# Cross-attention stage of a one-core encoder step: weight loads queued later, staging and operand buffers moved, first two score products no longer interleaved

## The chip, the core and the metric

The kernel runs on one core of one Trainium2 chip. The metric is the device time of one execution in microseconds (us). The kernel before takes 2992.53 us, the median of 3 runs (2989.19 to 2996.63). The names of the engines are those of the profile: PE is the matrix engine, DVE the vector engine, ACT the scalar engine, POOL the general engine, SP the engine that issues most of the transfers. Operands live in on-chip memory (SBUF), sums of matmuls in a small second memory (PSUM), the large arrays in DRAM.

## The reference

One layer of an encoder on 2048 prompt rows (16 tiles of 128 rows) and 128 sample rows (one more tile, S). Three sub-layers follow one another, each with a norm before and after it and an addition to its input:

```python
x = x + rmsnorm(mixer(rmsnorm(x, g_mix_pre)), g_mix_post)          # attention over a band, convolution, projection
x = x + rmsnorm(memory_attention(rmsnorm(x, g_mem_pre)), g_mem_post)  # 4 heads into 256 memory tokens
x = x + rmsnorm(ffn(rmsnorm(x, g_ffn_pre)), g_ffn_post)            # SwiGLU, hidden 2816

def memory_attention(h, mk, mv, w_mq, w_mo):
    q = (h @ w_mq)                                  # per head
    s = einsum("bthd,bmhd->bhtm", q, mk) * MEM_HEAD_DIM ** -0.5
    p = softmax(s, axis=-1)
    return einsum("bhtm,bmhd->bthd", p, mv) @ w_mo
```

## The kernel before, in words

The stages run one after another: memory keys and values, input projection, band attention, output projection of the mixer (`mixout`), cross attention (`phase_cross`), the first half of the feed-forward layer (`gate_up`) and the second (`down`). A tile scheduler puts the program's instructions into one list for each engine; an engine works through its list strictly in order and waits at each instruction for what that instruction needs. A buffer is a place in memory that a pool hands out in rotation, and an instruction that writes a buffer waits until the last reader of whatever lay at that place has finished. So two names that share a place are tied to each other even where no data passes between them.

A float32 product is made of three products of "high" and "low" parts. `mm3h` (L286 to L292) gives, for one 128-row slice k of the operands, six matmuls 128x512; a product of a tile with a 1024x1024 matrix is eight slices, 48 matmuls, all at L291.

**The end of `mixout` (L1030 to L1063).** It takes tile S and then tiles 0 to 15. For each it loads a tile of x (L1036), runs 48 matmuls, squares (ACT L1053), a small sum and a power on POOL (L1054, L300, L301), scales by the norm on DVE (L1057) into the single buffer `po`, adds x on POOL (L1058) and stores the result x1 by a transfer from POOL (L1059). Between these matmuls stands the whole cross attention of the sample rows (`cross_sample`), whose last piece is `postnorm` (L334 to L341: ACT L308, POOL L300 and L301, DVE L339, POOL L340, store L341). It uses the same buffer `po`.

**`phase_cross`.** Folded weights are kept in DRAM: `f1s` for the scores, `f2s` for the values, eight blocks each. `load` (L1207) brings one block into a staging buffer `stg` (there are three), ACT makes its high part (L1212), and DVE, or POOL for blocks 1, 3 and 5 of `f1`, makes the low part (L1213). `norm(t)` loads tile t of x1 (L1218) and runs `prenorm`: ACT square (L308), POOL L300 and L301, DVE scaling into the single buffer `hn` (L315), eight transposes on PE (L318) into the PSUM place `t`, the high part by ACT (L319), the low part by DVE (L320). `scores` makes 48 matmuls into a PSUM place, then a maximum on DVE (L1230), four exponentials on ACT (L1234), a reciprocal (L1237) and four scalings (L1239). `probs` transposes the result on PE (L1245) into the same place `t` and splits it (ACT L1248, DVE L1249). `values` makes 48 matmuls and calls `postnorm`.

In the steady part the program order for tile t is: transposes of the probabilities of t, scores of t+1, norm of t+2, values of t. From t = 4 on, `natural` (L1263 to L1285) is called once a tile as long as there is work for it: it takes two finished tiles of the cross stage and prepares the operands of the feed-forward stage. It loads the two tiles into `na` and `nb` (L1270), squares (ACT L1273), POOL L1275 and L1276, scales each (DVE L1277), makes four differences on POOL (L1278, L1280, L1282, L1284) and stores four pieces to the DRAM array `hn` with transfers that POOL issues (L1279 `na`, L1281 `nt`, L1283 `nb`, L1285 `na` again).

**The opening of `phase_cross`.** The program calls `norm(0)`, the eight loads of `f1`, `norm(1)`, `scores` of tile 0 into the PSUM place `y`, then two loads of `f2` behind the first exponentials, then `probs` and the scores of tile 1. The scheduler interleaves the scores of tiles 0 and 1.

**The opening of `gate_up`.** The first weights of the feed-forward layer come into four buffers `wf`; `wforms` derives four sums from them on POOL (L1372 to L1375), and splits seven forms on ACT (L1377) and DVE (L1378). `tform` loads pieces of `hn` and transposes them on PE (L1355; ACT L1357, DVE L1358). The products are L283, L284 and L285 (128x384).

**Places in memory.** The tables `lay(arena, start, (name, size, count))` and `at(name, size, (arena, [starts]))` give the places, in units of 1 KB a partition. In the float32 arena `sbF` of `phase_cross`: `stg` at 0, 4, 8; `gpre` 12; `junk` 16; `hn` 18; `xt` 22, 26, 30. `na`, `nb` and `nt` are laid at 0, 4, 8, over the staging buffers that are done by then. `gate_up` uses in the same arena `wf` at 12, 18, 46.5, 22, `s` (the derived sums) at 26, 28, 38.5, and `x1`, `x2` at 30, 31.5, 33, 34.5.

Of the kernel before, what the change touches and what calls it, by code (L numbers as in the profile page):

```python
# [20 lines left out]
NPT = 16  # L21
# [37 lines left out]
def halves(y):  # L59
    return [y[:, o, :] for o in range(2)]  # L60
# [76 lines left out]
class Build:  # L137
# [149 lines left out]
    def mm3h(self, y, lh, ll, rh, rl, start, stop):  # L287
        nc = self.nc
        for x, (l, r) in enumerate(((lh, rh), (lh, rl), (ll, rh))):
            for o in range(2):  # L290
                nc.tensor.matmul(y[o], l, r[:, o * 512:(o + 1) * 512], start=start and x == 0,  # L291
                                 stop=stop and x == 2)  # L292

    def rstd(self, pool, ss, scale):
        nc = self.nc
# [683 lines left out]
    def mixout(self, ctx):  # L979
# [52 lines left out]
        for i, t in enumerate(order):  # L1032
            mh, ml = ready.pop(t)
            pre = ahead(i)
            xt = self.t(pool, [P, D], F32, "xt", 2)
            nc.sync.dma_start(xt[:, :], self.rows("x", t))  # L1036
            y = [self.t(ps_y, [P, 512], F32, "y")[:, :] for _ in range(2)]
            for k in range(KC):
                self.mm3h(y, mh[:, k, :], ml[:, k, :], ws[k][0], ws[k][1], k == 0, k == KC - 1)
# [21 lines left out]
                fill, due = self.cross_sample(pool, ps_so, ps_p), 0.0  # L1061
        for _ in fill:
            pass  # L1063

    def cross_sample(self, pool, ps_so, ps_p):
        nc, A = self.nc, self.A
# [121 lines left out]
    def phase_cross(self, ctx):  # L1188
        nc, A = self.nc, self.A
        sbF, sbR = self.sbF, self.sbR  # L1190
        fr = Joined(*self.flex(ctx, *[(1024, F32R)] * 11))
        pool = (Region().lay(sbF, 0, ("stg", 4, 3), ("gpre", 4, 1), ("junk", 2, 1), ("hn", 4, 1), ("xt", 4, 3))
                .lay(sbF, 34.5, ("gpost", 4, 1), ("z", 4, 2), ("po", 4, 1), ("ss", 0.015625, 6),
                     ("rstd", 0.015625, 6), ("nmx", 0.03125, 2), ("sm", 0.03125, 2), ("ri", 0.03125, 2))
                .at("sh", 4, (sbR, [44, 40, 24])).at("sl", 4, (sbR, [52, 48, 28]))
                .lay(sbF, 0, ("na", 4, 1), ("nb", 4, 1), ("nt", 4, 1)))
        for k, o in enumerate((56, 64, 80, 0, 8, 16, 72, 88)):
            pool.lay(sbR, o, (f"f1{k}h", 4, 1), (f"f1{k}l", 4, 1))
        spots = [(sbR, o) for o in (32, 36, 96, 100, 104)] + [(fr, 4 * i) for i in range(11)]
        for i, (arena, o) in enumerate(spots):  # L1200
            pool.at(f"f2{i // 2}{'hl'[i % 2]}", 4, (arena, [o]))
        ps_t = ps_s = ps_y = (Region().at("y", 4, (self.ps, [4, 0])).lay(self.ps, 8, ("t", 4, 1), ("s", 4, 1)))
# [13 lines left out]
        def norm(t):  # L1216
            xt = self.t(pool, [P, D], F32, "xt", 4)
            nc.sync.dma_start(xt[:, :], self.x1[t])  # L1218
            hh = self.t(pool, [P, KC, P], F32R, "sh", 3)
            hl = self.t(pool, [P, KC, P], F32R, "sl", 3)  # L1220
            self.prenorm(pool, ps_t, xt, gpre, hh[:, :, :], hl[:, :, :], tag="t", keep=True)
            return xt, hh, hl

        def scores(hh, hl, where="s"):
            s = self.t(ps_s, [P, 2, 512], F32, where)
            for k in range(KC):
                self.mm3h(halves(s), hh[:, k, :], hl[:, k, :], f1[k][0], f1[k][1], k == 0, k == KC - 1)
            sv = s[:, :, :].rearrange("p a (h n) -> p (a h) n", n=NM)
            nmx = self.t(pool, [P, MH], F32, "nmx", 2)
            nc.vector.tensor_reduce(nmx[:, :], sv, axis=AX.X, op=ALU.max, negate=True)  # L1230
            z = self.t(pool, [P, MH, NM], F32, "z", 2)
            sm = self.t(pool, [P, MH], F32, "sm", 2)
            for h in range(MH):
                self.last_exp = nc.scalar.activation(z[:, h, :], sv[:, h, :], AF.Exp, bias=nmx[:, h:h + 1],  # L1234
                                                     accum_out=sm[:, h:h + 1])
            ri = self.t(pool, [P, MH], F32, "ri", 2)
            nc.vector.reciprocal(ri[:, :], sm[:, :])  # L1237
            for h in range(MH):
                nc.vector.tensor_scalar(z[:, h, :], z[:, h, :], ri[:, h:h + 1], None, ALU.mult)  # L1239
            return z  # L1240
# [21 lines left out]
        def natural(g, p):  # L1262
# [5 lines left out]
            for x, (t, r0) in zip((xa, xb), PAIRS[g][p][:2]):  # L1268
# [17 lines left out]

        self.natural = natural
        todo = [(g, p) for g in range(3) for p in range(3)]
        hq = {0: norm(0)}
        f1 = [load(self.f1s[:, k, :, :].rearrange("p h n -> p (h n)"), f"f1{k}",  # L1290
                   nc.gpsimd if k in (1, 3, 5) else nc.vector) for k in range(KC)]
        hq[1] = norm(1)
        z = scores(*hq[0][1:], "y")
        f2 = []

        def more(n, event):
            with self.tc.issue_after(event.ins):
                for k in range(len(f2), min(len(f2) + n, KC)):
                    f2.append(load(self.f2s[:, k, :], f"f2{k}"))

        more(F2, self.last_exp)
        for t in range(NPT):
            pp = probs(z) if t < NPT - 1 else self.last_probs
            if t == 0:
                more(KC, self.last_split)
            if t + 1 < NPT:
                z = scores(*hq[t + 1][1:])
            if t + 2 < NPT:
                hq[t + 2] = norm(t + 2)
            values(t, hq.pop(t)[0], *pp)  # L1310
            for g, p in list(todo):
                ready = all(x == S_TILE or x < t for x, _ in PAIRS[g][p][:2])
                if ready and t >= 4:
                    natural(g, p)
                    todo.remove((g, p))
                    break
# [333 lines left out]
```

## Time and profile before

| | |
|---|---|
| median of 3 runs | 2992.53 us (2989.19 to 2996.63) |
| the profiled execution, its own time | 2992.62 us |
| its span (first to last instruction) | 2990.8 us, mean granted clock of PE 0.987 |
| busy share of PE, DVE, ACT, POOL | 97%, 70%, 44%, 46% |
| norm of tile 0 to the end of the last values of the cross stage | about 1145 to 1566 us of the span |

A row of the timeline gives start, duration, engine, line, operation and what it writes and reads, and in brackets how long the engine had stood idle before it and what ended that. A row of the windows gives, for a stretch of the span, the busy time and number of instructions of each engine, the clock that PE was granted (1.00 is full speed), the share of the time in which the transfer engines moved data, and the rate. The waits give "engine, line <- what it waited for: total, times, longest" in us.

### The profile page before, as it was taken

To read this page: it belongs to the slowest core of one execution; us is meant where nothing else is said; L and a number is where in the kernel's file an instruction comes from. 1 tells how busy PE (TensorE), PEld (TensorE's weight loads), DVE (VectorE), ACT (ScalarE), POOL (GpSimd) and SP (SyncE) were. 2 spreads that over 40 slices of the span, in tenths; PEclk is the share of its full clock that TensorE was granted. 3 is DMA by queue.
4 is the path that set the end of the run, shared out by engine and by line. 5 is a ranking of instruction groups with operands and counts; after the bars stand their busy time and mean duration, and the time that the engine had idled before them with its cause. 6 is when DMAs were issued, how large, how long until landed. Compare 5 with 4: busy or idle time off the path is not lost.

```text
span 2990.8 us, 45392 instructions
## 1 busy us (share of the span) xinstructions
PE 2893.6 (97%) x16740; PEld 2636.6 (88%) x16740; DVE 2083.7 (70%) x3023; ACT 1314.1 (44%) x2665; POOL 1368.1 (46%) x1244
## 2 busy tenths in 40 slices
PE   8999999979989998999999999999999999999998
PEld 7999999959977777788878999999999999888786
DVE  6697895958975344435459878788888998555655
ACT  4535465648973223333334333433344444433433
POOL 0267496720013223135347656455556776424413
PEclk9999999989999999999999999999999999999999
DMA  8735255557844664224246333544434446756664
GB/s 300 247 115 176 97 167 159 176 151 189 207 134 157 233 212 169 71 88 146 96 156 218 132 126 131 187 144 159 148 128 150 150 145 213 241 171 221 220 193 165
DMA packets 198474, 500.04 MB, mean 167 GB/s; under 512 B 18981, under 2 KB 87085, under 8 KB 189923
## 3 DMA queue, kind: packets, MB, share of 16 engines
q1 hardware_dynamic: 187931, 461.09, 47.9%
q0 software_dynamic: 10320, 36.05, 3.1%
q8 instruction: 131, 2.15, 0.3%
q14 instruction: 92, 0.75, 0.1%
HBM read 365.97 MB, written 141.81 MB: 170 GB/s over the span
## 4 chain that ended last, share of the span: by engine, by line
PE 41%; DMA 4%; POOL 3%; DVE 2%; issue 2%; ACT 0%; DVEq 0%; SPq 0%; POOLq 0%; ACTq 0%
PE psb L285 13%; PE psb L284 13%; PE psb L283 13%; DMA sbf<-in_w_down_dram 1%; PE psb L291 1%; POOL sbf L1500 1%; DMA sbf<-x 1%; PE psb L1355 1%; DMA sbf<-hn 1%; POOL sbf L340 0%; DVE sbr L1561 0%; DMA sbf<-af 0%; DVE sbr L1378 0%; DMA hn<-sbf 0%; DVE flexb L1440 0%
## 5 line engine op out<-in xcount | busy, mean ns | idle before, releaser
L283 PE MATMUL psb<-sbr 128*128 128x384 f32 (+3 forms) x2808 | 943.1, 337 | 5.3 <-ACT sbr L1560 1.9
L284 PE MATMUL psb<-sbr 128*128 128x384 f32 (+3 forms) x2356 | 806.2, 342 | 2.4 <-DVE sbr L320 2.4
L285 PE MATMUL psb<-sbr 128*128 128x512 f32 (+3 forms) x1848 | 633.0, 344 | 2.8 <-DVE sbr L1561 2.6
L283 PEld LDWEIGHTS psb<-sbr 128*128 128x128 f32 x2808 | 531.0, 189 | 34.9 <-ACT sbr L1560 2.8
L285 PE MATMUL psb<-sbr,sbx 128*128 128x384 f32 (+2 forms) x1484 | 477.4, 322 | 0.0
L284 PEld LDWEIGHTS psb<-sbr 128*128 128x128 f32 x2356 | 445.6, 189 | 29.2 <-DVE sbr L320 2.7
L285 PEld LDWEIGHTS psb<-sbr 128*128 128x128 f32 x1848 | 347.9, 189 | 32.0 <-DVE sbr L1561 5.2
L291 PE MATMUL psb<-sbr 128*128 128x512 f32 x1200 | 299.6, 401 | 14.4 <-DVE flexb L1057 5.3
L1378 DVE TENSOR_TENSOR sbr<-sbf,sbr 128x512 fp32r<-128x512 f32 x258 | 263.5, 1024 | 38.6 <-ACT sbr L1377 37.8
L291 PEld LDWEIGHTS psb<-sbr 128*128 128x128 f32 x1200 | 227.6, 193 | 67.4 <-DVE flexb L1057 5.5
L1377 ACT CAST sbr<-sbf 128x512 fp32r<-128x512 f32 x258 | 159.3, 620 | 278.0 <-PE psb L284 225.1
L285 PEld LDWEIGHTS psb<-sbr,sbx 128*128 128x128 f32 x1484 | 281.1, 190 | 0.2
L523 DVE SCALAR_TENSOR_TENSOR psb<-sbf,psb 128x768 f32<-128x768 f32 (+1 forms) x290 | 264.3, 911 | 6.2
L1561 DVE TENSOR_TENSOR sbr<-sbf,sbr 128x384 fp32r<-128x384 f32 (+1 forms) x231 | 164.1, 734 | 91.3 <-ACT sbr L1560 90.2
L278 POOL TENSOR_TENSOR sbx<-sbf,sbr 128x1024 fp32r<-128x1024 f32 x60 | 152.5, 2545 | 79.4 <-ACT sbr L277 75.1
L1500 POOL TENSOR_TENSOR sbf<-sbf 128x512 f32<-128x512 f32 x77 | 107.0, 1395 | 167.4 <-DMA sbf<-in_w_down_dram 165.7
L1560 ACT CAST sbr<-sbf 128x384 fp32r<-128x384 f32 (+1 forms) x231 | 110.7, 497 | 163.8 <-PE psb L284 138.7
L533 POOL TENSOR_TENSOR flexb<-flexb,flexb 128x128 f32<-128x128 f32 (+1 forms) x180 | 167.5, 931 | 21.4 <-ACT flexb L532 11.9
L283 PE MATMUL psb<-sbr,sbx 128*128 128x384 f32 (+1 forms) x524 | 170.5, 327 | 0.7 <-ACT sbr L1357 0.7
L1377 ACT CAST sbx<-sbf 128x512 fp32r<-128x512 f32 x153 | 94.7, 620 | 160.9 <-PE psb L284 145.8
L1378 DVE TENSOR_TENSOR sbx<-sbf,sbx 128x512 fp32r<-128x512 f32 x153 | 153.9, 1008 | 14.5 <-ACT sbx L1377 14.3
L277 ACT CAST sbr<-sbf 128x1024 fp32r<-128x1024 f32 x98 | 102.4, 1049 | 103.5 <-PE psb L284 55.9
(319 smaller groups left out, 5936.8 us busy)
## 6 DMA issues: line engine op xcount, KB each, us to landing
af<-flexb SPq DMA_DIRECT2D x33, 1344.0 KB, 6.1
sbf<-in_w_down_dram SPq DMA_DIRECT2D x154, 256.0 KB, 3.8
sbf<-af SPq DMA_DIRECT2D x90, 384.0 KB, 4.2
sbf<-in_w_gate_dram SPq DMA_DIRECT2D x66, 512.0 KB, 3.3
sbf<-in_w_up_dram SPq DMA_DIRECT2D x66, 512.0 KB, 3.4
sbf<-x SPq DMA_DIRECT2D x49, 512.0 KB, 4.0
sbf<-in_w_in_dram SPq DMA_DIRECT2D x48, 512.0 KB, 3.9
sbr<-ks SPq DMA_DIRECT2D x28, 512.0 KB, 9.7
```

The lines of the kernel that those rows point to most:

```text
L278: self.lo_engine.tensor_tensor(lo[:, :], wf[:, :], hi[:, :].bitcast(F32), ALU.subtract)
L283: nc.tensor.matmul(ps, lh, rh, start=start, stop=False, **kw)
L284: nc.tensor.matmul(ps, lh, rl, start=False, stop=False, **kw)
L285: nc.tensor.matmul(ps, ll, rh, start=False, stop=stop, **kw)
L291: nc.tensor.matmul(y[o], l, r[:, o * 512:(o + 1) * 512], start=start and x == 0, stop=stop and x == 2)
L523: nc.vector.scalar_tensor_tensor(acc if w < CW - 1 else o, src(w), cwt[:, j, w:w + 1], acc, ALU.mult, ALU.add)
L533: nc.gpsimd.tensor_tensor(o, o, v, ALU.add)
L1377: nc.scalar.copy(hs[j][:, :], src[j])
L1378: nc.vector.tensor_tensor(ls[j][:, :], src[j], hs[j][:, :].bitcast(F32), ALU.subtract)
L1500: nc.gpsimd.tensor_tensor(acc[:, :], acc[:, :], q[:, :], ALU.add if s > 0 else ALU.subtract)
L1560: nc.scalar.copy(ch[:, m], a[:, x, m])
L1561: nc.vector.tensor_tensor(cl[:, m], a[:, x, m], ch[:, m].bitcast(F32), ALU.subtract)
```

## The change

Four things are done.

1. `mixout` keeps its last load of x, and the norm of tile 0 and the eight loads of `f1` are issued only behind it.
2. The scores of tile 0 now run whole in the PSUM place `s`, with the norm of tile 1 (its transposes too) put before their fourth slice. The scores of tile 1 follow whole in `y`, with the transposes of the first probabilities put inside. The first two `f2` loads are no longer tied to the first exponentials; the other six are tied to those of tile 0.
3. The places in memory change. In `sbF`: `stg` 0, 8, 16; `hn` 4; `gpre` 12; `xt` 24, 28, 20; `junk` 32. The operands `sh` and `sl` and the blocks of `f1` and `f2` move in their arenas as well. The lines that lay `na`, `nb`, `nt` at 0, 4, 8, and those of `gate_up`, stay as they are; `nb` now has the place of `hn`, `s` at 26 and the `wf` at 22 and 18 lie over `xt`.
4. `mm3h` remembers its last matmul, for the ties of point 2.

From L1194 on lines move by 3 to 15: the loads of `f1` and `f2` are L1212 (L1209 before), their low parts L1216 (L1213), the transposes of the probabilities L1252 (L1245), the loads of `natural` L1277 (L1270), its stores L1286, L1288, L1290, L1292, the transposes of `tform` L1370 (L1355), the sums of `wforms` L1387 to L1390 (L1372 to L1375).

```diff
--- before.py
+++ after.py
@@ -288,8 +288,8 @@
         nc = self.nc
         for x, (l, r) in enumerate(((lh, rh), (lh, rl), (ll, rh))):
             for o in range(2):
-                nc.tensor.matmul(y[o], l, r[:, o * 512:(o + 1) * 512], start=start and x == 0,
-                                 stop=stop and x == 2)
+                self.last_half = nc.tensor.matmul(y[o], l, r[:, o * 512:(o + 1) * 512], start=start and x == 0,
+                                                  stop=stop and x == 2)
 
     def rstd(self, pool, ss, scale):
         nc = self.nc
@@ -1033,7 +1033,7 @@
             mh, ml = ready.pop(t)
             pre = ahead(i)
             xt = self.t(pool, [P, D], F32, "xt", 2)
-            nc.sync.dma_start(xt[:, :], self.rows("x", t))
+            last_x = nc.sync.dma_start(xt[:, :], self.rows("x", t))
             y = [self.t(ps_y, [P, 512], F32, "y")[:, :] for _ in range(2)]
             for k in range(KC):
                 self.mm3h(y, mh[:, k, :], ml[:, k, :], ws[k][0], ws[k][1], k == 0, k == KC - 1)
@@ -1061,6 +1061,7 @@
                 fill, due = self.cross_sample(pool, ps_so, ps_p), 0.0
         for _ in fill:
             pass
+        self.last_x = last_x
 
     def cross_sample(self, pool, ps_so, ps_p):
         nc, A = self.nc, self.A
@@ -1189,14 +1190,16 @@
         nc, A = self.nc, self.A
         sbF, sbR = self.sbF, self.sbR
         fr = Joined(*self.flex(ctx, *[(1024, F32R)] * 11))
-        pool = (Region().lay(sbF, 0, ("stg", 4, 3), ("gpre", 4, 1), ("junk", 2, 1), ("hn", 4, 1), ("xt", 4, 3))
+        pool = (Region().at("stg", 4, (sbF, [0, 8, 16])).at("hn", 4, (sbF, [4])).at("gpre", 4, (sbF, [12]))
+                .at("xt", 4, (sbF, [24, 28, 20])).at("junk", 2, (sbF, [32]))
                 .lay(sbF, 34.5, ("gpost", 4, 1), ("z", 4, 2), ("po", 4, 1), ("ss", 0.015625, 6),
                      ("rstd", 0.015625, 6), ("nmx", 0.03125, 2), ("sm", 0.03125, 2), ("ri", 0.03125, 2))
-                .at("sh", 4, (sbR, [44, 40, 24])).at("sl", 4, (sbR, [52, 48, 28]))
+                .at("sh", 4, (sbR, [88, 48, 24])).at("sl", 4, (sbR, [92, 52, 28]))
                 .lay(sbF, 0, ("na", 4, 1), ("nb", 4, 1), ("nt", 4, 1)))
-        for k, o in enumerate((56, 64, 80, 0, 8, 16, 72, 88)):
+        for k, o in enumerate((64, 80, 0, 8, 16, 72, 56, 40)):
             pool.lay(sbR, o, (f"f1{k}h", 4, 1), (f"f1{k}l", 4, 1))
-        spots = [(sbR, o) for o in (32, 36, 96, 100, 104)] + [(fr, 4 * i) for i in range(11)]
+        spots = ([(sbR, o) for o in (32, 36, 96, 100, 104)] +
+                 [(fr, 4 * i) for i in (7, 8, 9, 10, 6, 4, 3, 2, 5, 1, 0)])
         for i, (arena, o) in enumerate(spots):
             pool.at(f"f2{i // 2}{'hl'[i % 2]}", 4, (arena, [o]))
         ps_t = ps_s = ps_y = (Region().at("y", 4, (self.ps, [4, 0])).lay(self.ps, 8, ("t", 4, 1), ("s", 4, 1)))
@@ -1221,13 +1224,17 @@
             self.prenorm(pool, ps_t, xt, gpre, hh[:, :, :], hl[:, :, :], tag="t", keep=True)
             return xt, hh, hl
 
-        def scores(hh, hl, where="s"):
+        def scores(hh, hl, where="s", mid=None):
             s = self.t(ps_s, [P, 2, 512], F32, where)
             for k in range(KC):
+                if mid and k == mid[0]:
+                    mid[1]()
                 self.mm3h(halves(s), hh[:, k, :], hl[:, k, :], f1[k][0], f1[k][1], k == 0, k == KC - 1)
             sv = s[:, :, :].rearrange("p a (h n) -> p (a h) n", n=NM)
             nmx = self.t(pool, [P, MH], F32, "nmx", 2)
-            nc.vector.tensor_reduce(nmx[:, :], sv, axis=AX.X, op=ALU.max, negate=True)
+            top = nc.vector.tensor_reduce(nmx[:, :], sv, axis=AX.X, op=ALU.max, negate=True)
+            if mid:
+                self.tc.keep_in_program_order(top)
             z = self.t(pool, [P, MH, NM], F32, "z", 2)
             sm = self.t(pool, [P, MH], F32, "sm", 2)
             for h in range(MH):
@@ -1286,25 +1293,33 @@
 
         self.natural = natural
         todo = [(g, p) for g in range(3) for p in range(3)]
-        hq = {0: norm(0)}
-        f1 = [load(self.f1s[:, k, :, :].rearrange("p h n -> p (h n)"), f"f1{k}",
-                   nc.gpsimd if k in (1, 3, 5) else nc.vector) for k in range(KC)]
-        hq[1] = norm(1)
-        z = scores(*hq[0][1:], "y")
-        f2 = []
-
-        def more(n, event):
-            with self.tc.issue_after(event.ins):
-                for k in range(len(f2), min(len(f2) + n, KC)):
-                    f2.append(load(self.f2s[:, k, :], f"f2{k}"))
-
-        more(F2, self.last_exp)
+        with self.tc.issue_after(self.last_x.ins):
+            hq = {0: norm(0)}
+            f1 = [load(self.f1s[:, k, :, :].rearrange("p h n -> p (h n)"), f"f1{k}",
+                       nc.gpsimd if k in (1, 3, 5) else nc.vector) for k in range(KC)]
+        f2 = [load(self.f2s[:, k, :], f"f2{k}") for k in range(F2)]
+
+        def second():
+            hq[1] = norm(1)
+
+        def opening():
+            ready[0] = probs(z)
+
+        ready = {}
+        with self.tc.issue_after(self.last_half.ins):
+            z = scores(*hq[0][1:], mid=(3, second))
+        first = self.last_half
+        with self.tc.issue_after(self.last_exp.ins):
+            f2 += [load(self.f2s[:, k, :], f"f2{k}") for k in range(F2, KC)]
         for t in range(NPT):
-            pp = probs(z) if t < NPT - 1 else self.last_probs
             if t == 0:
-                more(KC, self.last_split)
-            if t + 1 < NPT:
-                z = scores(*hq[t + 1][1:])
+                with self.tc.issue_after(first.ins):
+                    z = scores(*hq[1][1:], "y", (5, opening))
+                pp = ready.pop(0)
+            else:
+                pp = probs(z) if t < NPT - 1 else self.last_probs
+                if t + 1 < NPT:
+                    z = scores(*hq[t + 1][1:])
             if t + 2 < NPT:
                 hq[t + 2] = norm(t + 2)
             values(t, hq.pop(t)[0], *pp)
```

On PE, from the second half of the products of tile 15 of `mixout` to the first values of the cross stage, this stood before (L318 twice: transposes of tiles 0 and 1; `sbr` and `sbx` are two parts of the operand memory; 79 and the rows behind it are the interleaved scores of tiles 0 and 1):

```order
L291 MATMUL psb<-sbr 128x512 x24
L318 MATMUL psb<-ident_73,sbf 128x128 x8
L291 MATMUL psb<-sbr 128x512 x25
L318 MATMUL psb<-ident_73,sbf 128x128 x8
L291 MATMUL psb<-sbr 128x512 x79
L291 MATMUL psb<-sbx,sbr 128x512 x6
L291 MATMUL psb<-sbr 128x512 x4
L291 MATMUL psb<-sbx,sbr 128x512 x6
L1245 MATMUL psb<-ident_73,sbf 128x128 x8
L291 MATMUL psb<-sbr 128x512 x4
L318 MATMUL psb<-ident_73,sbf 128x128 x8
```

And this stands there now:

```order
L291 MATMUL psb<-sbr 128x512 x48
L318 MATMUL psb<-ident_73,sbf 128x128 x8
L291 MATMUL psb<-sbr,sbx 128x512 x8
L318 MATMUL psb<-ident_73,sbf 128x128 x8
L291 MATMUL psb<-sbr,sbx 128x512 x40
L291 MATMUL psb<-sbr 128x512 x38
L1252 MATMUL psb<-ident_73,sbf 128x128 x8
L291 MATMUL psb<-sbr 128x512 x14
L318 MATMUL psb<-ident_73,sbf 128x128 x8
```

The transposes of tile 0 stood between the two halves of tile 15 of `mixout` and now stand behind both; the scores of tile 0 are 8 and 40 matmuls around the transposes of tile 1, and those of tile 1 are 38 and 10 around the probabilities of tile 0.

On PE in the steady part, in the tiles in which `natural` runs, before (values of one tile with the transposes L318 of the tile after next, then the first two matmuls of the next scores and the probabilities; `flexb` numbers name blocks of `f2`):

```order
L291 MATMUL psb<-sbx,sbr 128x512 x2
...
L318 MATMUL psb<-ident_73,sbf 128x128 x8
...
L291 MATMUL psb<-flexb_10332,sbr 128x512 x2
L291 MATMUL psb<-sbr 128x512 x2
L1245 MATMUL psb<-ident_73,sbf 128x128 x8
L291 MATMUL psb<-sbr 128x512 x40
```

And now, in values of tiles 5, 7, 11 and 13:

```order
L291 MATMUL psb<-flexb_10300,sbx 128x512 x2
L291 MATMUL psb<-flexb_10296,sbx 128x512 x2
L291 MATMUL psb<-flexb_10300,sbx 128x512 x2
L318 MATMUL psb<-ident_73,sbf 128x128 x8
L291 MATMUL psb<-sbr 128x512 x4
L1252 MATMUL psb<-ident_73,sbf 128x128 x8
```

The transposes L318 stood after 20 of the 48 matmuls of the values, with 30 matmuls between them and the probabilities; in these four tiles they stand behind all 48, with four matmuls between. In the values of tiles 6 and 12 they stand after 38, of 8 after 46, of 9 and 10 after 17 and 20, of the others after 20 or fewer as before.

On DVE the scaling L315 of seven tiles now also waits for a transfer that POOL issued (a name DMASW among its waits), which it did for no tile before. One of them, with the rows ahead of it (L1235, L1244 and L1246 are the softmax, L339 and L320 as before):

```order
L1235 TENSOR_REDUCE sbf<-psb 128x4 [waits PE_49]
L1244 RECIPROCAL sbf<-sbf 128x4 [waits Activation_49]
L1246 TENSOR_SCALAR sbf<-sbf 128x256 [waits DVE_49]
L1246 TENSOR_SCALAR sbf<-sbf 128x256 x3
L315 SCALAR_TENSOR_TENSOR sbf<-sbf 128x1024 [waits DMAHW4_49,DMASW2_49,Pool_49]
L339 SCALAR_TENSOR_TENSOR sbf<-psb,sbf 128x1024 [waits DMASW0_49,Activation_49,Pool_49]
L320 TENSOR_TENSOR sbr<-psb,sbr 128x1024 [waits Activation_49]
```

Behind the waiting L315 stand L339 and L320 of the same stretch. In turn the load of `nb` (L1277, on SP) now waits for the transposes L318 that read `hn`.

On POOL, at the end of the cross stage, before (x_13, x_14 and x_15 are the finished tiles; L1372 to L1375 are the sums of the first feed-forward block):

```order
L340 TENSOR_TENSOR sbf<-sbf 128x1024
L341 DMA x_13_67_139<-sbf 128x1024
L1372 TENSOR_TENSOR sbf<-sbf 128x512
L1373 TENSOR_TENSOR sbf<-sbf 128x512
L1374 TENSOR_TENSOR sbf<-sbf 128x512
L1375 TENSOR_TENSOR sbf<-sbf 128x512
L300 TENSOR_SCALAR sbf<-sbf 128x1
L301 TENSOR_TENSOR sbf<-sbf,mhalf_78 128x1
L340 TENSOR_TENSOR sbf<-sbf 128x1024
L341 DMA x_14_68_140<-sbf 128x1024
```

And now, from the last cross tile on:

```order
L340 TENSOR_TENSOR sbf<-sbf 128x1024
L1282 TENSOR_SCALAR sbf<-sbf 128x1
L1286 DMA hn_73_145<-sbf 128x1024
L1387 TENSOR_TENSOR sbf<-sbf 128x512
L341 DMA x_15_69_141<-sbf 128x1024
L1283 TENSOR_TENSOR sbf<-sbf,mhalf_78 128x1
L1388 TENSOR_TENSOR sbf<-sbf 128x512
L1389 TENSOR_TENSOR sbf<-sbf 128x512
L1390 TENSOR_TENSOR sbf<-sbf 128x512
```

The four sums stood behind the addition L340 of tile 13, two tiles ahead of the end; they stand behind that of tile 15 now.

## Prediction

> **What bounds the kernel now.** The page first: how much of the span is PE work, and so how much any change of order can win.
>
> ```profile
> span 2990.8 us, 45392 instructions
> PE 2893.6 (97%) x16740; PEld 2636.6 (88%) x16740; DVE 2083.7 (70%) x3023; ACT 1314.1 (44%) x2665; POOL 1368.1 (46%) x1244
> ```
>
> The change leaves the PE work as it is (the same matmuls in another order), so it can only win PE's idle time and the time in which its clock is low, and only where it moves something: from about 1150 us (last tile of the mixer) to about 1620 us (first feed-forward blocks). The windows show where, in the opening:
>
> ```profile
> 1150.00:1160.00 10.00, 5.20 (x28) 4.17 (x26) 4.68 (x4) 2.99 (x8) 6.19 (x9) 0.93 0.45 157
> 1160.00:1170.00 10.00, 8.01 (x24) 6.08 (x24) 2.33 (x3) 3.49 (x5) 5.77 (x6) 0.73 0.52 161
> 1170.00:1180.00 10.00, 8.14 (x26) 6.25 (x27) 9.30 (x7) 4.14 (x5) 5.73 (x4) 0.66 0.53 174
> ...
> 1190.00:1200.00 10.00, 8.21 (x38) 6.45 (x37) 3.21 (x6) 3.03 (x10) 0.00 (x0) 1.00 0.07 30
> 1200.00:1210.00 10.00, 7.38 (x28) 5.86 (x27) 9.22 (x14) 6.63 (x14) 0.00 (x0) 0.66 0.55 170
> ```
>
> The first numbers behind the length are PE's busy us and matmuls. In these five stretches PE is idle for 13.1 us (4.8, 2.0, 1.9, 1.8, 2.6). The column behind the five engines is the granted clock: 0.73, 0.66, 0.66 after idle stretches. Granted time lost is 10 x (0.07 + 0.27 + 0.34 + 0.34) = 10.2 us, of which the share in which PE worked, about 8 us. So the opening can give back at most 13.1 + 8 = 21 us. PE's own waits there, longest first:
>
> ```profile
> PE psb L291 <- DVE flexb L1057: 5.3, 1, 5.3
> PE psb L291 <- ACT sbr L1212: 2.7, 1, 2.7
> PE psb L291 <- ACT sbr L1248: 2.6, 1, 2.6
> PE psb L1245 <- DVE sbf L1239: 1.8, 1, 1.8
> ```
>
> The largest is followed back on POOL and SP:
>
> ```profile
> 1147.48 2.40 POOL L1213 TENSOR_TENSOR sbr<-sbf,sbr 128x1024 fp32r<-128x1024 f32 x1
> 1149.96 1.05 POOL L300 TENSOR_SCALAR flexb<-flexb 128x1 f32<-128x1 f32 x1
> ...
> 1156.59 0.63 POOL L341 DMA_DIRECT2D x<-flexb  x1 [0.30 <-POOL flexb L340]
> 1161.19 2.36 POOL L1058 TENSOR_TENSOR flexb<-flexb 128x1024 f32<-128x1024 f32 x1 [3.98 <-DVE flexb L1057]
> 1163.58 0.33 SPq L1036 DMA_DIRECT2D flexb<-in_x_prompt_dram  x1
> 1160.49 8.01 PE L291 MATMUL psb<-sbr 128*128 128x512 f32 x24 [5.29 <-DVE flexb L1057]
> ```
>
> A low part of `f1` (L1213) sits on POOL ahead of tile S's norm (L300), which delays the sample rows' store (L341), that holds the buffer `po`, that L1057 of tile 14 needs, that PE's second half of tile 15 needs.
>
> **The change part by part. A, the opening.** Without `f1` on POOL, L300 of tile S can start when its square is done, about 1147.8 instead of 1149.96, and the small instructions behind it are no longer held either: the sum is 3 us earlier for L341, L1057 and PE's second half (1160.49 becomes about 1157.4). The transposes of tile 0, some 1.0 us of cover, have left the space ahead of it: PE waits from about 1154.2, 3.2 us. What is late next: the norm of tile 0. Its load goes behind tile 15's load of x, that waits for L1058 of tile 14 (1163.58 less 3: about 1160.6), and lands about 5.4 us later by these rows, in which a load alone takes 3.6 us and ACT starts on it at once:
>
> ```profile
> 1173.92 0.32 SPq L1209 DMA_DIRECT2D sbf<-f1s  x1
> 1177.52 1.04 ACT L1212 CAST sbr<-sbf 128x1024 fp32r<-128x1024 f32 x1 [3.64 <-DMA sbf<-f1s]
> ```
>
> The load of x ahead and its own 0.3 us of issue add the rest. Square, POOL, L315 (1.1 + 0.8 + 1.3 us and hand-overs) bring the transposes to about 1169.5; PE has finished tile 15 at about 1164: 5 us idle. Then L319 (1.0 us) stands alone ahead of the scores: 1.3 us. They start at about 1172. All eight `f1` blocks are now loaded here through three staging buffers: 3.6 us load, 1.05 us cast, 1.2 us (DVE) to 2.4 us (POOL) low part, 5.9 to 7.1 us a turn, so a block every 2.0 to 2.4 us, where PE would need one every 1.4 us (six matmuls at 0.23 us, from this row: 28 in 6.5 us).
>
> ```profile
> 1352.82 1.09 PE L318 MATMUL psb<-ident,sbf 128*128 128x128 f32 x8
> 1353.67 6.62 PE L291 MATMUL psb<-flexb,sbr 128*128 128x512 f32 x28
> 1360.14 0.62 PE L291 MATMUL psb<-sbr 128*128 128x512 f32 x2
> 1360.60 1.03 PE L1245 MATMUL psb<-ident,sbf 128*128 128x128 f32 x8
> ```
>
> Block 0 is ready at about 1172, block 7 seven turns later, 1186 to 1189, plus its own six matmuls; with a low clock after these idle stretches I take 1192 for the end of the scores of tile 0 (bounds 1187 and 1197). From there to the probabilities of tile 2 stand 48 matmuls four times over less two (values 0, values 1, scores 1 and 2: 44 us), 8 transposes four times (4.1 us) and the first hand-over of the split (0.9 us): about 49.5 us with a pair of scores of tile 3, so 1241.5. Before they started here:
>
> ```profile
> 1242.92 1.03 PE L1245 MATMUL psb<-ident,sbf 128*128 128x128 f32 x8
> ```
>
> So A is -1 us, between -6 and +4: the waits for L1239 and L1248 go (the probabilities have 38 matmuls of cover now), but waits for the norm of tile 0 and for `f1` come.
>
> **B, `natural` over `hn`.** In the steady part before, PE waits for nothing but this, in four tiles:
>
> ```profile
> PE psb L318 <- DVE sbf L315: 3.7, 4, 1.5
> ```
>
> Now `nb` lies on `hn`. How long `nb` is held, from one tile's rows (load, the next tile's scaling, store, and the landing of the store):
>
> ```profile
> 1335.58 1.04 SPq L1270 DMA_DIRECT2D sbf<-x  x2
> 1350.47 2.30 DVE L315 SCALAR_TENSOR_TENSOR sbf<-sbf 128x1024 f32<-128x1024 f32 x1 [1.06 <-POOL sbf L301]
> 1356.99 0.61 POOL L1283 DMA_DIRECT2D hn<-sbf  x1
> DMA to landing us min/median/max: 3.0/3.0/3.0
> ```
>
> That is 1335.6 to 1360.0, 24.4 us, about a whole tile, and L315 came 9.5 us before the end of it. It can now come only behind 1360.0, and end 1.3 to 2.3 us later, while the values without the transposes inside would end at about 1359.1. If `natural` kept its times, PE would wait 2.2 to 3.2 us; if the scheduler's new order starts its work early enough, nothing. I take 0.9 us, nearer to nothing, since the rows' pure work (3.7 load, 1.1 square, 1.3 to 3.4 scaling, 4.7 differences, 3.0 store) is only some 14 to 16 of the 24 us. What is sure is the order: in four tiles L318 stands right ahead of its user. Two rows price that:
>
> ```profile
> L319 ACT CAST sbr<-psb 128x1024 fp32r<-128x1024 f32 x13 | 13.3, 1023 | 8.0 <-PE psb L318 8.0
> L320 DVE TENSOR_TENSOR sbr<-psb,sbr 128x1024 fp32r<-128x1024 f32 x13 | 15.8, 1217 | 6.0 <-ACT sbr L319 5.9
> ```
>
> PE waits for L319, 1.0 us and 0.3 us of hand-over, runs four matmuls (0.9 us), and waits for L320 to clear the place `t`, 1.2 + 0.3 - 0.9 = 0.6 us. That is 0.9 + 1.3 + 0.6 = 2.8 us a tile, 11.2 us in four, and 1.2 us in values 8 (two matmuls of cover); the 3.7 us of before are gone with them: B is +8.7 us. Bounds: 4 x 1.9 less 3.7 is +4, at 3.2 us of lateness each +18.
>
> **C, the feed-forward opening.** The four sums of the first block ran early before, under the cross stage, and can now only follow the addition of tile 15:
>
> ```profile
> 1536.71 1.30 POOL L1372 TENSOR_TENSOR sbf<-sbf 128x512 f32<-128x512 f32 x1
> ...
> 1541.04 1.74 POOL L1375 TENSOR_TENSOR sbf<-sbf 128x512 f32<-128x512 f32 x1
> 1569.89 2.38 POOL L340 TENSOR_TENSOR sbf<-sbf 128x1024 f32<-128x1024 f32 x1
> 1566.04 0.34 PE L283 MATMUL psb<-sbr 128*128 128x384 f32 x1
> 1570.00:1580.00 10.00, 6.84 (x39) 5.53 (x39) 8.47 (x10) 4.58 (x10) 8.06 (x7) 1.00 0.86 280
> 1580.00:1590.00 10.00, 8.53 (x43) 7.43 (x44) 6.47 (x10) 5.01 (x9) 8.03 (x9) 0.83 0.83 274
> 1590.00:1600.00 10.00, 10.00 (x64) 9.92 (x63) 10.00 (x11) 5.14 (x9) 8.78 (x6) 1.00 0.93 305
> ```
>
> They took 6.1 us there (1536.71 to 1542.8). Now the second product's form comes after 1572.3, two transfers and a power (1.7 us) and two sums (2.6 us): 1576.6, and 1.6 us of splitting behind. The first product starts at 1566 and has with its transposes some 5 us of work, to about 1571. That is some 6 us of waiting where before 3.2 us stood idle up to 1580: +3. The other two sums push the next block back on a POOL that is busy 8 of 10 us, while DVE is full from 1590 on: another +2. C is +5 us, between 0 (the transposes moved ahead fill the wait) and +12 (all 6.1 us on both blocks).
>
> **Sum.** -1 + 8.7 + 5 = +12.7 us on 2992.62 us of the profiled execution, 3005.3. The median of the runs is 0.1 us from that execution, so the forecast is 3005 us. About 0.3%, 9 us, is what a measurement of this kernel tells from no change.
>
> **The rivals.** *The opening pays (faster).* If loads of `f1` come quicker than one in 1.4 us, the scores of tile 0 are bound by PE and end about 1184, the clock stays up, and A is 1184 + 49.5 - 1242.9 = -9, with one low stretch less -12; if B and C also find cover (0 to +3), 2982. For it: three transfers at a time, and DVE is idle most of 1180 to 1190 before. Against it: three buffers at 5.9 us a turn cannot beat 2.0 us. It decides at a block every 1.4 us. Chance 0.08.
>
> *The side effects are hidden (no change).* `natural` keeps ahead, the stalls of B are only the +4, the sums are covered, A between -6 and 0: 2994. For it: 8 us of slack in a tile. Chance 0.25.
>
> *The clock goes down with the stalls.* In the opening the clock fell to 0.66 and 0.73 behind waits of 2.6 to 5.3 us, and not behind those of 1.5 us of the steady part. Two waits of B with the transposes between them are 2.2 to 2.8 us idle within 4 us: if that is enough, each of four tiles runs a stretch of 3.4 to 6.8 us at half speed (the low stretches of the opening are of about this length: 10 us at 0.66 are 6.8 us at half), 1.7 to 3.4 us each: +7 to +14, so 3012 to 3019. Chance 0.17. The Trainium skill, "TensorE: Matmul & The Clock Gate", section "HAM oscillation — how this bites in real kernels", says that gaps of PE beyond some 3.4 us throttle it, each time anew. By that rule this rival would not come, since each gap is shorter; the trace disagrees in part, for 2.6 us idle ahead of 1203.58 were enough:
>
> ```profile
> 1203.58 2.07 PE L291 MATMUL psb<-sbr 128*128 128x512 f32 x4 [2.62 <-ACT sbr L1248]
> ```
>
> Four matmuls in 2.07 us are half speed.
>
> **How the numbers follow.** The forecast's own case has 0.50 (3001 to 3010), the rivals 0.08, 0.25 and 0.17. Slower by over 0.3% (above 3001.5) takes the forecast and the clock rival: 0.67; within 0.3%: 0.25; faster: 0.08. The range of 8 in 10 leaves out the faster rival, the end of the clock rival and a little of the no-change case: 2993 to 3018.
>
> **What would show it.** In the profile after: PE's wait for L1057 near 3 us; a wait L318 for L315 near 5 us at about 1165; waits for L1215 or L1216 of 3 to 7 us in the scores of tile 0; the probabilities of tile 2 at about 1241; waits for L319 in four or five tiles of the steady part, with L320 behind; the probabilities of tile 14 about 8 us later than before against those of tile 2; POOL L1387 behind 1572 and a wait of the second product. It is wrong if the scores of tile 0 end before 1185, if L315 never waits for a store, or if the feed-forward opening is as before.

## The result, and the profile after

The changed kernel takes 3012.2 us (median of 4, 3009.42 to 3015.31) against 2990.86 us before (4 runs): ratio 1.0068, 95% interval 1.0052 to 1.0084, so 15.6 to 25.1 us slower. Forecast were 3005 us, range 2993 to 3018.

One profiled execution of each (spans 2990.8 and 3013.5 us), cut at events that both have, in us:

| stretch | before | after | difference |
|---|---|---|---|
| start to the store of tile 13 of x1 (L1059) | 1139.9 | 1143.7 | +3.8 |
| A: to the probabilities of tile 2 (L1245, now L1252) | 103.0 | 104.3 | +1.3 |
| B: to the probabilities of tile 15 | 307.6 | 317.0 | +9.4 |
| C: to the first store L1450 (L1465) after the first turn of the feed-forward stage | 410.2 | 418.8 | +8.6 |
| to the end | 1030.1 | 1029.8 | -0.3 |

The first row is no effect of the change: but for a load or two that SP issues in its last 2 us, both run the same instructions there, and the twelve profiles of the experiments put that store between 1136.1 and 1143.1 us. So single profiles carry some 4 us of their own, and A, B and C, 19.3 us together, stand for the measured 0.68%, 20 us.

PE's waits between 1100 and 1300 us, after:

```profile
PE psb L318 <- DVE sbf L315: 7.0, 1, 7.0
PE psb L291 <- DVE sbr L1216: 4.5, 3, 2.4
PE psb L291 <- DVE flexb L1057: 2.6, 1, 2.6
PE psb L291 <- ACT sbr L1215: 2.1, 2, 1.8
PE psb L291 <- ACT sbx L319: 1.1, 1, 1.1
```

The waits of before for L1239 and L1248 are gone, that for L1057 is halved, and the norm of tile 0 (L315) and the `f1` blocks (L1215, L1216) took their place: 17.3 us in these rows, 12.4 in the four of before. The windows after show the price of the clock in the same place; its column follows the five engines:

```profile
1160.00:1170.00 10.00, 5.73 (x24) 4.43 (x24) 1.28 (x2) 0.07 (x1) 2.99 (x2) 0.97 0.50 155
1170.00:1180.00 10.00, 3.19 (x10) 2.07 (x10) 7.25 (x6) 7.68 (x12) 8.23 (x11) 0.50 0.39 159
```

In the steady part (1230 to 1566 us) there was one kind of wait, 3.7 us. Now:

```profile
PE psb L291 <- ACT sbr L319: 5.0, 5, 1.1
PE psb L318 <- DVE sbf L315: 2.8, 4, 0.9
PE psb L1252 <- DVE sbr L320: 1.9, 3, 0.7
```

One of these tiles in the timeline after: the store of `nb` on POOL, its landing by the view of that line, the scaling on DVE, and PE.

```profile
1387.22 0.61 POOL L1290 DMA_DIRECT2D hn<-sbf  x1
DMA to landing us min/median/max: 3.5/3.5/3.5
1390.81 1.29 DVE L315 SCALAR_TENSOR_TENSOR sbf<-sbf 128x1024 f32<-128x1024 f32 x1 [3.11 <-issue]
1392.16 1.09 PE L318 MATMUL psb<-ident,sbf 128*128 128x128 f32 x8 [0.90 <-DVE sbf L315]
1394.35 1.86 PE L291 MATMUL psb<-sbr 128*128 128x512 f32 x4 [1.10 <-ACT sbr L319]
```

1387.22 + 3.5 = 1390.7: L315 starts when the store has landed ("issue" is a wait that the profile does not name). Ahead of two other L315 the profile names the store itself, 10.3 us of idle time in sum (the last numbers of this row, whose window is 1230 to 1640 us):

```profile
L315 DVE SCALAR_TENSOR_TENSOR sbf<-sbf 128x1024 f32<-128x1024 f32 x13 | 16.7, 1285 | 66.9 <-POOL sbf L301 45.1 <-issue 11.5 <-DMA hn<-sbf 10.3
```

PE waits for L315, then for L319. The row of L291 also has four matmuls in 1.86 us where 0.23 each is full speed: here the clock fell.

The feed-forward opening: PE's longest waits before (5.7 us with the two smaller ones left out here), then after (11.1 us with one left out), then the rows of DVE, POOL and PE behind those for L1373 and for `hn`.

```profile
PE psb L1355 <- DMA sbf<-hn: 2.1, 2, 1.7
PE psb L1355 <- DVE sbr L1358: 1.8, 3, 1.0
PE psb L283 <- DVE flexb L1428: 0.8, 1, 0.8
```

```profile
PE psb L1370 <- DVE sbr L1373: 4.1, 3, 2.9
PE psb L283 <- DVE flexb L1443: 3.6, 1, 3.6
PE psb L1370 <- DMA sbf<-hn: 3.1, 1, 3.1
```

```profile
1585.04 2.35 POOL L340 TENSOR_TENSOR sbf<-sbf 128x1024 f32<-128x1024 f32 x1
1585.47 2.99 DVE L1284 SCALAR_TENSOR_TENSOR sbf<-sbf,flexb 128x1024 f32<-128x1024 f32 x1
1588.39 1.28 DVE L1373 TENSOR_TENSOR sbr<-psb,sbr 128x512 fp32r<-128x512 f32 x2
1589.12 1.94 PE L1370 MATMUL psb<-ident,sbf 128*128 128x128 f32 x8 [2.86 <-DVE sbr L1373]
1589.40 1.28 POOL L1387 TENSOR_TENSOR sbf<-sbf 128x512 f32<-128x512 f32 x1
1592.32 3.71 DVE L1393 TENSOR_TENSOR sbr<-sbf,sbr 128x512 fp32r<-128x512 f32 x1
1598.17 0.63 PE L1370 MATMUL psb<-ident,sbf 128*128 128x128 f32 x4 [3.06 <-DMA sbf<-hn]
```

The first sum, L1387, comes at 1589.4 behind L340, as the order says. But PE does not wait for the sums themselves: the order fills their time with transposes L1370, and these wait, for a PSUM place that L1373 clears only behind L1284, and for their own loads. The late sums also hold up DVE: the low part L1393 took 3.71 us from 1592.32, and 0.69 us in the same shape at 1579.37, while POOL made the other three sums from 1591.73 to 1595.48. What this row costs PE is not shown.

### The profile page after: what moved, and what is told of

It is laid out like the page before. It is cut to its first block, busy times and chain, and to the rows that moved or that the text cites. A ratio compares the mean times of both kernels' runs of the same rounds, so it can differ in the third digit from the quotient of the medians.

```text
span 3013.5 us, 45389 instructions
## 1 busy us (share of the span) xinstructions
PE 2899.8 (96%) x16740; PEld 2638.8 (88%) x16740; DVE 2077.3 (69%) x3023; ACT 1313.1 (44%) x2665; POOL 1356.9 (45%) x1244
## 5 line engine op out<-in xcount | busy, mean ns | idle before, releaser
L283 PEld LDWEIGHTS psb<-sbr 128*128 128x128 f32 x2808 | 531.9, 190 | 33.2 <-ACT sbr L319 1.5
L284 PEld LDWEIGHTS psb<-sbr 128*128 128x128 f32 x2356 | 446.5, 190 | 28.4 <-DVE sbr L320 2.7
L285 PEld LDWEIGHTS psb<-sbr 128*128 128x128 f32 x1848 | 348.5, 189 | 31.4 <-DVE sbr L1576 4.2
L1393 DVE TENSOR_TENSOR sbr<-sbf,sbr 128x512 fp32r<-128x512 f32 x258 | 262.6, 1020 | 43.6 <-ACT sbr L1392 42.6
L285 PEld LDWEIGHTS psb<-sbr,sbx 128*128 128x128 f32 x1484 | 281.4, 190 | 0.2
L291 PE MATMUL psb<-sbr 128*128 128x512 f32 x978 | 240.0, 397 | 10.8 <-ACT sbr L319 5.0
L291 PEld LDWEIGHTS psb<-sbr 128*128 128x128 f32 x978 | 182.2, 190 | 54.5 <-ACT sbr L319 6.4
L291 PE MATMUL psb<-sbr,sbx 128*128 128x512 f32 x782 | 197.9, 402 | 11.2 <-DVE sbr L1216 4.5
L291 PEld LDWEIGHTS psb<-sbr,sbx 128*128 128x128 f32 x782 | 146.3, 191 | 49.4 <-DVE sbr L1216 6.1
L1393 DVE TENSOR_TENSOR sbx<-sbf,sbx 128x512 fp32r<-128x512 f32 x153 | 158.2, 1035 | 15.9 <-ACT sbx L1392 15.4
```

The costliest lines, as they stand in the source:

```text
L283: nc.tensor.matmul(ps, lh, rh, start=start, stop=False, **kw)
L284: nc.tensor.matmul(ps, lh, rl, start=False, stop=False, **kw)
L285: nc.tensor.matmul(ps, ll, rh, start=False, stop=stop, **kw)
L291: self.last_half = nc.tensor.matmul(y[o], l, r[:, o * 512:(o + 1) * 512], start=start and x == 0, stop=stop and x == 2)
L1393: nc.vector.tensor_tensor(ls[j][:, :], src[j], hs[j][:, :].bitcast(F32), ALU.subtract)
```

## The experiments

Each was timed against the kernel before in five rounds; ratios to it, with the 95% interval.

| kernel | ratio | interval |
|---|---|---|
| changed kernel | 1.0068 | 1.0052 to 1.0084 |
| changed, `nb` off `hn` (e1) | 1.0032 | 1.0023 to 1.0041 |
| changed, old float32 arena (e3) | 1.0004 | 0.9992 to 1.0016 |
| before, `nb` on `hn` (e4) | 1.0039 | 1.0026 to 1.0052 |
| before, `xt` under the feed-forward buffers (e5) | 1.0029 | 1.0019 to 1.0039 |
| e5 with `xt` turned (p3) | 1.0019 | 1.0008 to 1.0029 |
| e3, norm of tile 0 not tied (o1) | 0.9997 | 0.9987 to 1.0006 |
| e3, nothing tied (o2) | 0.9967 | 0.9953 to 0.9980 |
| o2, low parts on DVE (o3) | 0.9972 | 0.9961 to 0.9982 |
| before, low parts on DVE (o5) | 1.0007 | 0.9997 to 1.0018 |
| before, new operand places only (p1) | 0.9942 | 0.9927 to 0.9958 |
| before, new order only (p2) | 1.0007 | 0.9999 to 1.0016 |
| p1 with the tie (p4) | 1.0011 | 0.9999 to 1.0022 |

**The side effects, one at a time.** e1: the changed kernel with

```diff
-.at("stg", 4, (sbF, [0, 8, 16])).at("hn", 4, (sbF, [4]))
+.at("stg", 4, (sbF, [0, 4, 8])).at("hn", 4, (sbF, [16]))
```

> The changed kernel with one thing different: the staging buffers lie at 0, 4, 8 and hn at 16, so that na, nb, nt share their places with staging only and no longer with hn. Theory (three separate costs: opening about +1 us, nb over hn about +9.4, feed-forward opening about +8.8): about 9 us less than the changed kernel's 3012, so 3003; the probabilities of tiles 2 and 15 307 to 308 us apart as before the change (317 with it); no wait of PE for L319 or L320 in the steady part; the feed-forward opening as late as in the changed kernel. Rival 1 (the loss is the opening's order, and the steady part's waits only follow from lateness that it hands on): 3010 to 3014. Rival 2 (most of the loss is contention of the engines in the natural tiles, not the place): the distance stays above 314 us and the time at 3010.

9.6 us above before, 10.8 below the changed kernel. The probabilities of tiles 2 and 15 are 307.8 us apart, PE waits for no L319 in the steady part, and the feed-forward opening stays late (C is 422.4 us in this profile). So B goes with the overlay.

e3: the changed kernel with the old line `lay(sbF, 0, ("stg", 4, 3), ("gpre", 4, 1), ("junk", 2, 1), ("hn", 4, 1), ("xt", 4, 3))`.

> The changed kernel with the old places in the float32 arena (stg 0, 4, 8, gpre 12, junk 16, hn 18, xt 22, 26, 30), all else as changed: the new order of the opening, the ties and the other arenas. Theory (opening +1, the rest is places): 2990 to 2994, the same as before. Rival 1 (the opening's order is the loss): 3005 to 3013. Rival 3 (the old places in the float32 arena hold up the opening's loads, which is what the new ones are for): the opening alone loses 5 us or more, so 2997 or above, with the probabilities of tile 2 later than in the changed kernel.

No difference from before (+1.2 us, -2.4 to +4.8): the loss is in the float32 places, and the opening, with its new order, operand places and ties together, costs and wins nothing that can be told.

e4: the kernel before with `stg` at 0, 8, 18 and `hn` at 4.

> The kernel before with one thing different: hn lies at 4 and the staging buffers at 0, 8, 18, so that nb shares its place with hn; order of the opening, xt and junk as before. Theory (the overlay alone costs about 9 us, by L318 right ahead of its users and by the wait of L315 for the store): 2999 to 3004, with five or more waits of PE for L319 of about 1.0 us and waits for L320 of 0.6 us between 1230 and 1566 us. Rival 1 (the opening's order is the loss): 2991. Rival 2 (contention, not the place): 2991 to 2994.

+11.7 us, a little above the expected size. The scheduler put the late transposes into more tiles than in the changed kernel, and its steady part waits for the same things:

```profile
PE psb L291 <- ACT sbr L319: 5.9, 6, 1.3
PE psb L1246 <- DVE sbr L320: 3.9, 4, 1.3
PE psb L318 <- DVE sbf L315: 2.2, 3, 1.0
```

e5: the kernel before with `stg` 0, 4, 8, `hn` 16, `xt` 24, 28, 20, `junk` 32.

> The kernel before with xt at 24, 28, 20, junk at 32 and hn at 16: the feed-forward buffers s and wf lie over the cross stage's last tiles as in the changed kernel, nb does not lie over hn, and the opening's order is that of before. Theory (the sums on POOL behind the last tile cost about 8.8 us): 2998 to 3002; the steady part without waits for L319; the act-form stores of the feed-forward stage 8 to 9 us later against the probabilities of tile 15 than before. Rival 1 (the opening's order is the loss): 2991. Rival 4 (the sums are covered by PE's own work and the loss behind tile 15 comes from elsewhere): 2991 to 2994.

+8.7 us, as expected; the steady part has the waits of before, and C is 422.4 us in this profile too. `hn` and `junk` move with `xt` here, so that `xt` alone carries the price is argued, not shown. p3 turns `xt` in it to 28, 24, 20.

> The run of the kernel before with xt at 24, 28, 20, with xt at 28, 24, 20 in its place: the last tile now lies over the second sum and not over the first, so two of the four sums (L1373, L1375 here) stand behind tile 14's addition and the other two still behind tile 15's. Theory (the sums behind the last tile are the price): between before and that run, 2994 to 3001, since the second product still needs the second sum. Rival (the price is the wf buffer over tile 14's xt, whose load waits): no less than that run's 3004.

+5.7 us, between before and e5, but the intervals of p3 and e5 meet: that half of the sums behind the last tile is a smaller price is likely by this and not shown.

e3, e4 and e5 add to 0.04 + 0.39 + 0.29 = 0.72%, the changed kernel has 0.68%.

**Why the opening won nothing.** In e3 the loss by places is gone, so its opening can be taken apart. o1 takes `norm(0)` out of the tie:

```diff
-        with self.tc.issue_after(self.last_x.ins):
-            hq = {0: norm(0)}
+        hq = {0: norm(0)}
+        with self.tc.issue_after(self.last_x.ins):
             f1 = [...]
```

> The run with the old places and the new order, with the norm of tile 0 no longer behind the last load of x; the eight f1 loads still are. Theory (in the new opening two things are late one behind the other, first the norm of tile 0, then the f1 blocks, at one block in some 2 us): the wait of L318 for L315 (5.4 us) goes, the transposes of tile 0 stand again between the halves of tile 15, but the first scores then wait for the first f1 block instead, so 1 to 4 us less than that run, 2991 to 2994. Rival (the norm of tile 0 is the whole loss): 7 to 8 us less, 2986 to 2988.

2 us below e3, as the theory had it, though the intervals of the two overlap: the wait for L315 is gone, and waits for L1214 and L1215 (7.7 us) stand there. o2 unties the loads too.

> The same with the f1 loads free as well, their low parts on POOL for blocks 1, 3 and 5 as before: the only thing left of the change is the scores whole and the probabilities inside. Theory: three f1 blocks come early as in the kernel before, POOL's low part stands ahead of tile S's norm again (wait for L1057 5 us), the later blocks come while the first scores run: 5 to 8 us less than with the ties, 2986 to 2990. Rival (the supply of f1 through three staging buffers binds either way): 2992 to 2995, with 4 us or more of waits for L1214 and L1215 in the scores of tile 0.

11 us below e3, more than expected: no wait for `f1` is left in the opening of o2, and PE's only two waits are 3.5 us for L1057 and 2.3 for L1254. The rival, that three staging buffers bind either way, falls. o3 and o5 make all low parts on DVE (`nc.vector` for `nc.gpsimd if k in (1, 3, 5) else nc.vector`), in o2 and in the kernel before.

> As the run without ties, with all low parts of f1 on DVE. Theory: no low part stands ahead of tile S's norm on POOL, so the wait for L1057 falls from 5 to about 3 us, and a turn of a staging buffer is 1.2 us shorter for three of the blocks: 2 to 5 us less than that run, 2982 to 2987. Rival (the wait for L1057 has another last cause, the transfer of tile S's result or the sums of tile 14): as that run within 1 us.

> The kernel before with all low parts of f1 on DVE and nothing else. Theory (the low part on POOL ahead of tile S's norm is what makes PE wait 5.3 us for L1057): this wait falls to about 3 us, the rest of the opening follows 2 us earlier: 2988 to 2991. Rival: no difference, as the wait has another last cause.

Both rivals hold: no difference. In o5 the wait for L1057 is still 5.6 us, and POOL shows why. The norm of tile S is early now (L339 starts at 1148.78), but its addition L340 stands behind others in POOL's order:

```profile
1149.95 0.19 POOL L300 TENSOR_SCALAR sbf<-sbf 128x1 f32<-128x1 f32 x1 [1.21 <-ACT sbf L308]
...
1151.09 0.19 POOL L1054 TENSOR_TENSOR flexb<-flexb 128x1 f32<-128x1 f32 x1 [0.32 <-ACT flexb L1053]
...
1152.16 2.35 POOL L340 TENSOR_TENSOR flexb<-flexb 128x1024 f32<-128x1024 f32 x1
```

A norm that waits for its load, and tile 14's sum, stand ahead of it; L339 is done at 1150.06, and L340 starts 2.1 us later. The low part was one cause, and taking it away uncovered the next.

o2 still had two parts of the change, the order and the operand places. p1 is the kernel before with the places alone, p2 has the order alone.

```diff
-.at("sh", 4, (sbR, [44, 40, 24])).at("sl", 4, (sbR, [52, 48, 28]))
+.at("sh", 4, (sbR, [88, 48, 24])).at("sl", 4, (sbR, [92, 52, 28]))
-for k, o in enumerate((56, 64, 80, 0, 8, 16, 72, 88)):
+for k, o in enumerate((64, 80, 0, 8, 16, 72, 56, 40)):
...
```

> The kernel before with only the new places of the operands sh, sl and of the blocks f1 and f2; order and float32 arena as before. Theory (the places in the operand arena let f1 blocks be written and multiplied while the mixing still holds its weights, so the third and later blocks come earlier; this and not the order is most of the 10 us that the run without ties gains): 2980 to 2985, the waits for L1212 in the first scores gone. Rival (the gain is the order: scores whole, probabilities inside): 2989 to 2993.

> The run without ties, with the old places of sh, sl, f1 and f2 too: what is left of the change is the scores whole and the probabilities inside. Theory (places make most of the gain): the first scores wait for f1 blocks as before, 2986 to 2990; the waits for L1239 and L1248 of before (1.8 and 2.6 us, with half clock behind) are gone, which is worth 4 us. Rival (the order is the gain): 2980 to 2983.

p1 is 17 us faster than before (12.6 to 21.8), more than expected, and the fastest of all: it beats both kernels. Stretch A of the table takes 86.1 us in its profile and 103.0 before, so the gain lies in the opening. p2 gains nothing, which neither its theory nor its rival had: its waits for L1239 and L1248 are gone, but 5.7 us for the cast of `f1` and 5.4 for L1057 are there. PE in p1, from the end of the first half of tile 15 on:

```profile
1154.92 1.03 PE L318 MATMUL psb<-ident,sbf 128*128 128x128 f32 x8
1157.06 0.73 PE L291 MATMUL psb<-sbr,sbx 128*128 128x512 f32 x2 [1.10 <-ACT sbx L319]
1158.47 1.09 PE L318 MATMUL psb<-ident,sbf 128*128 128x128 f32 x8 [0.68 <-DVE sbx L320]
1159.31 1.17 PE L291 MATMUL psb<-sbr,sbx 128*128 128x512 f32 x4
1160.33 5.62 PE L291 MATMUL psb<-sbr 128*128 128x512 f32 x24
```

Two tiles' transposes and the first scores now run where PE waited 5.3 us for L1057; the second half of tile 15 starts at 1160.33 without a wait, at full speed (24 in 5.62 us, 8.01 before). The tables say why they could not before: the old place of `f1` block 0, 56, is that of the mixer's last weight slice (L969), and `sh` at 44 lies on `ml` of tile 15; both are read up to its last matmul, and a sum of scores begins with block 0. The new places, 64 and 80 for blocks 0 and 1 and 88 for `sh`, are free once the sample rows' products and tile 14 are done. (The edit moves `f2` as well; no run moves one of the operands alone.) In the kernel before, the first matmul of the scores waits behind tile 15 for the cast of block 0:

```profile
1171.19 0.50 PE L291 MATMUL psb<-sbr 128*128 128x512 f32 x1 [2.69 <-ACT sbr L1212]
```

If so, a tie of norm and loads behind the last load of x must undo it. p4 adds this tie, and nothing else, to p1:

> The kernel before with the new places of sh, sl, f1 and f2 and, of the rest of the change, only the tie: the norm of tile 0 and the f1 loads behind the last load of x. Theory (the new places win by letting the first scores run inside PE's wait for L1057, which needs the norm of tile 0 and three f1 blocks early; the tie takes just these away): the 17 us of the run with the places alone are gone but for 0 to 4, 2989 to 2994, with PE waiting some 5 us for L315 ahead of the first transposes and 2 to 3 us for L1057. Rival (the places win by the supply of the later f1 blocks, which the tie leaves): 2978 to 2984.

It does: +3 us against before (0 to +7), 21 above p1. Its three longest waits stand in the changed kernel's opening too:

```profile
PE psb L318 <- DVE sbf L315: 5.4, 1, 5.4
PE psb L291 <- DVE sbr L1214: 2.4, 1, 2.4
PE psb L291 <- DVE flexb L1057: 2.2, 1, 2.2
```

So the opening of the change holds a gain and a tie that takes it back: 17 us in the old order (p1 and p4), and in the new order, that of the changed kernel, about 12 us (o2 against p2) of which the tie takes 11 (e3 against o2). With the places and no tie, the new order (o2) is 7 us behind the old one (p1), 0.25%, but their intervals just meet, and without the new places the order made no difference (p2). That interleaved scores fill each other's waits could explain the 7 us; it is not shown.

## Why the prediction was right, and where not

The sign, the three places and the side effects were right, the sum too small: +12.7 us against 20 (15.6 to 25.1).

- *A, -1 us; +1.3 in the profile, +1.2 in e3.* The times hold when the 3.8 us of the first row are taken off: transposes of tile 0 forecast at 1169.5, measured 1173.37 - 3.8 = 1169.6; end of the scores of tile 0 at 1192 (bounds 1187 to 1197), measured 1199.9 - 3.8 = 1196, 4 us late and near the upper bound. The step that failed is the cause of the first term: "Without `f1` on POOL, L300 of tile S can start" 2 us earlier, and PE's second half 3 us earlier. The 3 us came (tile 14's store at 1164.05 - 3.8 = 1160.3, 1163.85 before), but o5 shows that the low part alone gives nothing; a norm's L300 and L1054 stand ahead of L340 on POOL too, and the changed order has both behind it or done. So the term came out right by luck: its stated cause is not enough by itself.
- *What A did not price.* The move of `sh`, `sl`, `f1` and `f2` had no term. p1 gives it 17 us in the old order, p4 shows the tie taking it. The ceiling of 21 us held; the rival "the opening pays" set the wrong condition, a block of `f1` every 1.4 us. What p1 and p4 point to is whether scores can start inside the wait for L1057.
- *B, +8.7 us; +9.4 in the profile, 10.8 by e1, 11.7 by e4.* Right in mechanism and near in size: 0.9 us a tile for the lateness of L315 was forecast and 0.7 measured (2.8 in four), 1.3 for L319 and 1.1 measured (four times 1.10, and 0.6 in a fifth tile where 1.2 was forecast), 0.6 for L320 and 0.6 measured (1.9 in three). The waits of the steady part rose by 6.0 us (9.7 less 3.7); the low clock behind one tile (0.58 over the 4 us from 1394) is some 1.7 of the rest, and as much is not assigned.
- *C, +5 us; +8.6 in the profile, 8.7 by e5's time, 12.2 in the profiles of e1 and e5.* The term that was mis-sized, and the step that failed in it is the wait. It said that the second product would wait for the second sum (its own times give 7.2 us, 1576.6 + 1.6 - 1571, where it wrote some 6); the order avoided that with transposes, and these waited 7.2 us for DVE and for loads, with 3.6 us more for L1443 a block later. All waits from 1566 us on are 11.1 us against 5.7 before, 5.4 more. By an estimate from the windows, the granted clock makes up most of the rest: 0.96, 0.84 and 0.86 in the three windows of 10 us from 1580 and 0.96 over 1660 to 1700, against one window of 0.83 before, some 3 us. Why each of these waits is longer with the new places stays open.
- *The rivals.* The clock rival came in one tile of the four, not as a rule; in the opening the clock was low before and after (0.50 over 10 us now). The rival of hidden side effects fell with e4 and e5.

## What to carry to other kernels

Price every line of a table of places by what shared the place before and what shares it now: here one set of lines was worth -17 us, another +11 and a third +9, on 2992. Places that let work start earlier and a tie that starts it later can cancel; time each alone. When one instruction ahead of a critical one is taken off a queue, look at what stands next in that queue before giving it a price.

## What the runs showed of the hardware

DVE and POOL held each other up where both read on-chip memory: L1284 took 2.99 us from 1585.47 while L340 ran on POOL to 1587.39, and L315 of the same shape 1.29 us (above), and L1284 ended 1.1 us after L340. POOL waited in turn: the small L1282 behind L340 took 1.05 us, to the end of L1284, and 0.19 us at 1584.17. The Trainium skill, "SBUF — State Buffer", section "SBUF: two separate sides", describes a port pair that these two engines hold for a whole instruction; the trace agrees.

A wait of 1.1 us for L319 behind one of 0.9 us for L315 was enough, in one tile, for the granted clock to fall to half (four matmuls in 1.86 us), and in three others, with 0.56, 0.56 and 0.77 us for L315, not. The 2.6 us of idle time ahead of 1203.58 before did not stand alone either: 1.2 us of transposes part them from another 1.8 us ahead of 1199.73. Length alone does not decide it: in e4 waits of 1.28 us for L319 and 1.27 us for L320, one behind the other, left the clock at 1.00. The runs do not show what does.
